# Summing the seven Strassen products of two feed-forward stages in PSUM, with operand sums prepared in other stages

## The chip, the cores and the metric

The kernel runs on one core of one Trainium2 chip. The metric is the device time of one execution in microseconds (us), the median of several runs. A core has a matrix engine (TensorE, PE in the profile), VectorE (DVE), ScalarE (ACT) and GpSimd (POOL); SyncE (SP) issues the DMA transfers between the chip's main memory and the on-chip memory, SBUF. TensorE writes its results into PSUM, eight banks of 128 partitions by 512 float32; GpSimd and the DMA engines do not read it.

## What is computed

Two decoder layers on 1024 tokens of width 1024, in float32. Each has a token mixing part (one input projection, four groups of heads A to D, one output projection) and a gated feed-forward part of inner width 2816:

```python
def conv_glu_ffn(h, w_gate, w_up, conv_w, w_down):
    gate = causal_dwconv(h @ w_gate, conv_w)
    return (jax.nn.gelu(gate, approximate=True) * (h @ w_up)) @ w_down

for l in range(DEPTH):
    h = rms_norm(x, pre_mix_g[l])
    ...
    x = x + rms_norm(mix, post_mix_g[l])
    h = rms_norm(x, pre_ffn_g[l])
    y = conv_glu_ffn(h, w_gate[l], w_up[l], conv_w[l], w_down[l])
    x = x + rms_norm(y, post_ffn_g[l])
```

## The kernel before

**Products.** A float32 product is taken as three matmuls (`mm3`, lines 208 to 212): every operand is split into a rounded part and a remainder in the float32r type, and hi·hi, hi·lo and lo·hi are added up in PSUM. `split` (line 195) makes the parts: a cast on ScalarE (L197) and a subtraction (L198) on GpSimd, or on VectorE where the call says so.

Both feed-forward stages use Strassen's scheme in Winograd's form. A and B are cut into 2 x 2 blocks, and seven products take the place of eight:

```python
#   S1 = A21 + A22, S2 = S1 - A11, S3 = A11 - A21, S4 = A12 - S2,
#   T1 = B12 - B11, T2 = B22 - T1, T3 = B22 - B12, T4 = B21 - T2,
#   P = A11 B11, S2 T2, A12 B21, S3 T3, A22 T4, S1 T1, S4 B22 (in the order they are taken),
#   U2 = P0 + P1, U3 = U2 + P3, C11 = P0 + P2, C21 = U3 + P4, C22 = U3 + P5, C12 = U2 + P5 + P6.
```

**Stages of a layer.** The input projection (`proj_d`, then `group_d`, `proj_c`, `proj_a`, `proj_b`, gates) takes feature tiles of 48 matmuls each; a tile's weight is loaded by `load` (L192) and split by ScalarE and GpSimd one or two tiles ahead. Group D's chunks run among the projections. Then come the groups A to C, the output projection and the two stages in question.

**Up stage** (`ffn1`, line 1229). A is the normed stream h (halves of tokens and of features). B is one tile f of 128 inner features, its gate and its up weights, for 22 tiles. `seq` lists (tile, product); every product is 12 matmuls of 512 columns into a PSUM bank of its own (pool pd, four banks). `prep` runs six products ahead: `operand_b` (line 1209) makes T1 to T4 on GpSimd, L1213, and `split` the two parts. After a product VectorE adds it to what came before (L1328: into u2, u3, z); ScalarE copies product 0 to p1 (L1337). `conv` runs the three taps of the convolution on VectorE (L1301, L1303) and the gelu on ScalarE, and L1334 multiplies gate by up. One tile of the gated result, 512 KB, is stored to gd. At the start, `combine_s2` and `combine_a` make the sums S1 to S4 of the stream and their parts; A5 takes the slot of s2 and so waits until S4 has been made.

**Down stage** (`ffn2`, line 1379). A is the gated result, B the weights wdn. The first tile is taken plainly by 48 matmuls. Nine pairs of tiles follow, in three groups of three (`PAIRS`); for a group each of the seven products is summed over its three pairs in four banks (one for each 128 tokens of a half) and then added by VectorE into acc or y in SBUF (L1395, in `op`). VectorE also makes S1 to S4 of each pair and GpSimd T1 to T4 (`operand_b`), four operands ahead (`NLA2`), from loads of 1 MB. The last three tiles are taken plainly by token tile, 18 matmuls each, with the post norm (`squares`, `rstd2`, `post_res`) and, in layer 0, the next layer's pre norm and its transposes (`prenorm_steps`, L219) following each token tile.

The order on each engine is fixed by a scheduler when the kernel is built; each engine takes its instructions in that order and waits on semaphores. Buffers are pools with a number of slots: a load or a write waits until the slot's last reader is done.

## Time and profile before

| | us |
|---|---|
| median of 3 runs | 3053.49 (3052.45 to 3054.06) |
| profiled execution, span | 3048.2 |
| TensorE busy | 2770.0 (91%) |
| VectorE busy | 2041.5 (67%) |
| GpSimd busy | 1690.1 (55%) |
| ScalarE busy | 1226.0 (40%) |

The span is that of one profiled execution, from its first to its last instruction. Matmuls are pipelined in the profile: one of 512 columns is shown with 0.39 us though the next starts 0.23 us later, so a busy TensorE isn't TensorE at its peak. "Clock" is the share of TensorE's full clock that the chip granted. A group of rows joins instructions of one line, operation and shape; "idle before, releaser" is the time in which the engine had waited, and whose instruction ended the wait. Names are those of the program's tiles without their numbers.

In layer 0 the up stage runs from about 787 to 1245 us and the down stage to about 1537; in layer 1 from 2306 to 2764 and to 3037.5.

### The profile page before, as it was taken

The numbers are of one execution on the slowest core, as the hardware profiler recorded it, in microseconds if no ns is written. First come the engines' busy times: TensorE is split into PE (matmuls) and PEld (weight loads), VectorE is DVE, ScalarE is ACT, GpSimd is POOL, SyncE is SP. The second block draws the span as 40 slices with busy tenths as digits, with TensorE's granted clock in tenths as the row PEclk, the third lists the DMA queues.
The fourth block names the chain that finished last, engine by engine and source line by source line (L and its number), as shares of the span: only waits on it lengthen the run. The fifth ranks groups of instructions, "written<-read, shape, count | busy, mean of one in ns | idle before, by whom it ended". The sixth has DMA issues, their size and how long they took to land. (4 is left out here: it accounts for less than half of the span.)

```text
span 3048.2 us, 39804 instructions
## 1 busy us (share of the span) xinstructions
PE 2770.0 (91%) x14952; PEld 2236.5 (73%) x14952; DVE 2041.5 (67%) x2866; ACT 1226.0 (40%) x2342; POOL 1690.1 (55%) x1362
## 2 busy tenths in 40 slices
PE   7999998999699999788899999989996999998878
PEld 6787775777588888666677877757775888886666
DVE  5564328863887777867855633388649877777787
ACT  4423437455433333333344234374544333334332
POOL 2121234546888887567631212344468988876684
PEclk9999999999899999889999999999998999999999
DMA  3221331124222222322222213311242222213223
GB/s 119 68 87 49 113 123 53 52 91 145 76 99 81 83 80 73 132 83 83 90 85 75 86 46 113 117 59 46 98 139 83 104 77 83 78 68 118 90 76 131
DMA packets 93551, 270.62 MB, mean 89 GB/s; under 512 B 17296, under 2 KB 28848, under 8 KB 93360
## 3 DMA queue, kind: packets, MB, share of 16 engines
q1 hardware_dynamic: 93360, 268.09, 25.6%
q8 instruction: 118, 1.93, 0.3%
q14 instruction: 73, 0.60, 0.1%
HBM read 203.50 MB, written 64.55 MB: 88 GB/s over the span
## 5 line engine op out<-in xcount | busy, mean ns | idle before, releaser
L198 POOL TENSOR_TENSOR wr<-wst,wr 128x512 fp32r<-128x512 f32 (+1 forms) x260 | 460.4, 1778 | 561.9 <-ACT wr L197 542.8
L211 PE MATMUL pd<-h,wr 128*128 128x512 f32 x1216 | 483.9, 398 | 0.6 <-DVE h L198 0.6
L210 PE MATMUL pd<-h,wr 128*128 128x512 f32 x1040 | 417.1, 401 | 0.0
L212 PE MATMUL pd<-h,wr 128*128 128x512 f32 x1040 | 414.2, 398 | 0.0
L197 ACT CAST wr<-wst 128x512 fp32r<-128x512 f32 (+1 forms) x262 | 198.1, 760 | 426.5 <-POOL wst L1213 131.7
L211 PEld LDWEIGHTS pd<-h,wr 128*128 128x128 f32 x1216 | 229.9, 189 | 54.0 <-issue 3.1
L1303 DVE SCALAR_TENSOR_TENSOR g<-z,pp,g 128x512 f32<-128x512 f32 x176 | 236.2, 1342 | 13.7 <-POOL z L1298 2.6
L210 PEld LDWEIGHTS pd<-h,wr 128*128 128x128 f32 x1040 | 195.8, 188 | 46.9 <-issue 5.1
L212 PEld LDWEIGHTS pd<-h,wr 128*128 128x128 f32 x1040 | 195.7, 188 | 44.0 <-issue 1.9
L210 PE MATMUL pd<-wr,h 128*128 128x256 f32 x640 | 185.5, 290 | 0.0
L211 PE MATMUL pd<-wr,h 128*128 128x256 f32 x640 | 184.8, 289 | 0.0
L212 PE MATMUL pd<-wr,h 128*128 128x256 f32 x640 | 184.5, 288 | 0.0
L210 PE MATMUL pd<-h 128*128 128x512 f32 x312 | 129.2, 414 | 59.0 <-DVE y L1395 52.5
L198 POOL TENSOR_TENSOR wr<-ust,wr 128x512 fp32r<-128x512 f32 x88 | 142.5, 1620 | 51.1 <-ACT wr L197 50.9
L215 PE MATMUL pm<-g,g 128*128 128x128 f32 (+1 forms) x672 | 118.2, 323 | 29.3 <-issue 12.9
L211 PE MATMUL pd<-hs,wr 128*128 128x512 f32 x352 | 139.0, 395 | 0.4 <-DVE hs L198 0.4
L210 PE MATMUL pd<-hs,wr 128*128 128x512 f32 x352 | 139.0, 395 | 0.0
L212 PE MATMUL pd<-hs,wr 128*128 128x512 f32 x352 | 138.6, 394 | 0.0
L215 PEld LDWEIGHTS pm<-g,g 128*128 128x128 f32 x672 | 97.0, 198 | 56.4 <-issue 30.9
L211 PE MATMUL pd<-h 128*128 128x512 f32 x312 | 127.1, 407 | 3.9 <-POOL h L198 3.9
L210 PEld LDWEIGHTS pd<-wr,h 128*128 128x128 f32 x640 | 125.6, 196 | 2.3 <-ACT t L378 1.5
L212 PE MATMUL pd<-h 128*128 128x512 f32 x312 | 126.3, 405 | 0.0
(418 smaller groups left out, 7422.1 us busy)
## 6 DMA issues: line engine op xcount, KB each, us to landing
wst<-in_wgu_dram SPq DMA_DIRECT2D x44, 512.0 KB, 3.5
ust<-in_wgu_dram SPq DMA_DIRECT2D x44, 512.0 KB, 3.5
gd<-g SPq DMA_DIRECT2D x44, 512.0 KB, 2.6
wst<-in_wfm_dram SPq DMA_DIRECT2D x32, 512.0 KB, 3.6
wst<-in_wo_dram SPq DMA_DIRECT2D x32, 512.0 KB, 3.6
x<-x SPq DMA_DIRECT2D x24, 512.0 KB, 4.2
wst<-in_wtm_dram SPq DMA_DIRECT2D x20, 512.0 KB, 3.6
h<-gd SPq DMA_DIRECT2D x10, 1024.0 KB, 7.9
```

The source lines that it names most:

```text
L197: self.marks["hi"] = self.nc.scalar.copy(out=hi, in_=src)
L198: (eng or self.nc.gpsimd).tensor_tensor(out=lo, in0=src, in1=hi.bitcast(F32), op=ALU.subtract)
L210: mm(out, lhsT=a[0], rhs=b[0], start=start, stop=False)
L211: mm(out, lhsT=a[0], rhs=b[1], start=False, stop=False)
L212: return mm(out, lhsT=a[1], rhs=b[0], start=False, stop=stop)
L215: self.nc.tensor.matmul(out, lhsT=lhsT, rhs=rhs, start=start, stop=stop)
L1303: nc.vector.scalar_tensor_tensor(out=c, in0=x[:, j:j + 512], scalar=w(j), in1=c, op0=ALU.mult, op1=ALU.add)
```

## The change

- `mm3` gets an argument `onto`, for adding onto a bank that has been read already.
- **Up stage.** Product 0 and then 1, 3 and 4 are added up in one bank (`pa`), products 5 and 6 in another (`pc`); ScalarE copies the bank after products 0, 1, 3 and 4, VectorE reads PSUM for products 2, 6 and 3 or 5. `seq` is in a new order that puts a product of another tile, or another bank, between two that share one. From the 13th product on, the remainder of five of the seven weight operands is made by VectorE instead of GpSimd. `combine_a` makes the parts of A5 earlier and in another slot. `store` writes the gated result of two tiles as the seven operands A11, S2, A12, S3, A22, S1, S4 (256 KB each), with four sums on VectorE; the last two tiles are written plainly.
- **Weight operands of the down stage.** `down_sums`, ten steps in each layer, run in the projection stage: two loads of 512 KB, four subtractions on GpSimd, two stores of 512 KB to td.
- **Down stage.** Ten pairs and two plain tiles. The product is the outer loop (0, 2, 1, 5, 6, 3, 4), the pairs the inner one; products 0, 1, 3, 4 share the four pm banks, 2 has pd banks, 5 and 6 share pd banks. The banks are emptied once per product. A class `Back` prepares operands, four ahead: two loads of 256 KB into a staging slot (four slots), one cast and one subtraction of 128 x 1024. The last six operands are taken by token tile. The next layer's norms use pd banks.

```diff
+    def mm3(self, out, a, b, start, stop, onto=False):
+        mm = lambda x, y, **k: self.nc.tensor.matmul(out, lhsT=x, rhs=y, skip_group_check=onto, **k)
...
+        self.td, self.sums = self.down_sums(l)
         cx = self.proj_c(l, hT, misc)
...
             self.proj_fm(l, hT, (AQ0 + i, evac))
+            next(self.sums, None)
...
-            A[3], A[4] = ((fr("f1", "hs", 4), fr("f1", "hs", 4)) for _ in range(2))
+            A[3], A[5] = ((fr("f1", "hs", 4), fr("f1", "hs", 4)) for _ in range(2))
...
-        seq = [(f, i) for i in (0, 2) for f in range(NFB)] + [(f, i) for f in range(NFB) for i in (1, 3, 4, 5, 6)]
-        seq += [(f, i) for f in range(NFB, NF) for i in range(7)]
+        seq = [(0, 0), (1, 0), (0, 2), (1, 2), (0, 1), (0, 3), (0, 5), (1, 1), (0, 4), (0, 6), (1, 5), (1, 3)]
+        for f in range(2, NF):
+            seq += [(f, 0), (f - 1, 4), (f - 1, 6), (f, 2), (f, 1), (f, 5), (f, 3)]
+        seq += [(NF - 1, 4), (NF - 1, 6)]
...
-            self.split(w[:, 0, :], w[:, 1, :], self.operand_b(i, *B[f]), nc.vector if j in LOV else None)
+            self.split(w[:, 0, :], w[:, 1, :], self.operand_b(i, *B[f]), nc.vector if j in LOV or j > 12 and i not in (0, 2) else None)
...
+            op(s1, a21, a22, ALU.add)
+            op(a21, a11, a21, ALU.subtract)
+            op(s2, a22, a21, ALU.subtract)
+            op(s4, a12, s2, ALU.subtract)
+            for i, x in ((1, s2), (3, a21), (5, s1), (6, s4)):
+                out(i, x)
...
+            if i == 0:
+                p = pa[f] = self.ps([128, 512], "pd" if f < 2 else "pm")
+            elif i == 5:
+                p = pc[f] = self.ps([128, 512], "pm" if f < 2 else "pd")
+            elif i == 2:
+                p = self.ps([128, 512], "pd")
+            else:
+                p = pc[f] if i == 6 else pa[f]
...
+            if i in (0, 1, 3):
+
+                x = xs[f, i] = self.t("f0", "x", 6, [128, 512])
+                nc.scalar.copy(out=x, in_=p)
+                if i == 3 and f in pc:
+                    nc.vector.tensor_tensor(out=x, in0=pc[f], in1=x, op=ALU.add)
...
-            for t in range(4):
-                self.mm3(ps[t], tuple(A[:, e, t * 128:(t + 1) * 128] for e in range(2)),
-                         tuple(B[:, e, :] for e in range(2)), k == 0, k == len(groups[gi]) - 1)
-                if k < len(groups[gi]) - 1:
-                    continue
...
-                    op(dve, x(i), x(i), ps[t], ALU.add)
...
+            for t in range(4):
+                self.mm3(banks[which][t], (X[:, 0, t * 128:t * 128 + 128], X[:, 2, t * 128:t * 128 + 128]),
+                         (X[:, 1, :], X[:, 3, :]), k and i in (0, 2, 5), stop, i in (1, 3, 4, 6))
+            if not stop:
+                continue
+            for t in range(4):
+                p = banks[which][t]
+                if i == 0:
+                    nc.scalar.copy(out=y[t][:, lo], in_=p)
+                elif i == 2:
+                    add(y[t][:, lo], p, y[t][:, lo])
+                    half(t, 0)
...
+            for p in range(NP):
+                w = [self.t("p1", "d", ND) for _ in range(2)]
+                for e in range(2):
+                    nc.sync.dma_start(out=w[e], in_=self.I["wdn"][l, 2 * p + e])
+                (b11, b12), (b21, b22) = ((x[:, 0:512], x[:, 512:1024]) for x in w)
+                sub = lambda o, x, y: nc.gpsimd.tensor_tensor(out=o, in0=x, in1=y, op=ALU.subtract)
+                sub(b11, b12, b11)
+                sub(b12, b22, b12)
+                sub(b22, b22, b11)
+                sub(b21, b21, b22)
+                for e in range(2):
+                    nc.sync.dma_start(out=td[p][:, 2 * e:2 * e + 2, :].rearrange("p a b -> p (a b)"), in_=w[e])
+                yield
...
+        self.seq = [(i, u) for i in (0, 2, 1, 5, 6, 3, 4) for u in pairs + (tail if i in (2, 6, 4) else [])]
...
+        r = b.t(*(("st", "st", 4) if self.more else ("w", "wst", 2)), [128, 2, 512])
...
+            dma(out=r[:, 0, :], in_=a)
+            dma(out=r[:, 1, :], in_=w)
+            X = b.t(*(("u", "u", NUL) if i == 4 else ("h", "h", 8)), [128, 4, 512], F32R)
+            b.split(X[:, 0:2, :], X[:, 2:4, :], r, b.nc.vector)
...
+NP, NU, NUL, NFIN = 10, 4, 4, 6
```

**What moves, on VectorE in the down stage of layer 0.** Before, at the end of a product of the first group. The rows with L1395 on r, h and ext are operand sums, L198 remainders, and y with pd the adds of the finished banks:

```order
L1395 TENSOR_TENSOR ext_10382<-r_10383 128x512
L1395 TENSOR_TENSOR r_10383<-r_10383 128x512
L1395 TENSOR_TENSOR h_10323<-h_10323,h_10322 128x512
L198 TENSOR_TENSOR h_10366<-h_10322,h_10366 128x512
L1395 TENSOR_TENSOR h_10325<-h_10325,h_10322 128x512
L1395 TENSOR_TENSOR r_10383<-r_10383,ext_10382 128x512
...
L198 TENSOR_TENSOR wr_10585<-ext_10382,wr_10585 128x512
L198 TENSOR_TENSOR wr_10605<-h_10323,wr_10605 128x512
L1395 TENSOR_TENSOR y_10380<-y_10380,pd_10567 128x512
L1395 TENSOR_TENSOR y_10380<-y_10380,pd_10568 128x512
```

After, at the end of product 2 (L198 on h and st is the remainder of one whole operand, L1452 the add of a bank, L232 a step of the norm):

```order
L198 TENSOR_TENSOR h_10887<-st_10884,h_10887 128x1024
L198 TENSOR_TENSOR h_10929<-st_10926,h_10929 128x1024
L198 TENSOR_TENSOR h_10947<-st_10944,h_10947 128x1024
L1452 TENSOR_TENSOR y_10482<-pd_10688,y_10482 128x512
L198 TENSOR_TENSOR h_10965<-st_10962,h_10965 128x1024
L232 TENSOR_SCALAR s_1963_10903<-s_1963_10903 128x1
L1452 TENSOR_TENSOR y_10483<-pd_10689,y_10483 128x512
```

The operand sums are gone from this place, and the remainders, of twice the size, stand one to an operand.

**On SP in the projection stage of layer 0.** wst is a weight of the projections (wst_3154 before and wst_3215 after is that of the second query tile of group A); C and A are stores of projected tiles, d loads of wdn and td stores of its sums. Before:

```order
L192 DMA wst_3081<-in_wfm_dram 128x1024
L1045 DMA od_1063<-do_2025 128x256
L697 DMA t_2910<-in_tab_dram 64x1024
L702 DMA kr_2915<-t_2909 64x1024
L192 DMA wst_3154<-in_wfm_dram 128x1024
L387 DMA C_2917<-t_2746 128x1024
```

After:

```order
L387 DMA C_2948<-t_2826 128x1024
L1528 DMA td_2687<-d_3117 128x1024
L1528 DMA td_2687<-d_3118 128x1024
L387 DMA A_3127<-t_3040 128x1024
L1520 DMA d_3190<-in_wdn_dram 128x1024
L1520 DMA d_3191<-in_wdn_dram 128x1024
L387 DMA A_3127<-t_3043 128x1024
L387 DMA A_3127<-t_3054 128x1024
L1528 DMA td_2687<-d_3190 128x1024
L1528 DMA td_2687<-d_3191 128x1024
L192 DMA wst_3215<-in_wfm_dram 128x1024
```

This weight stood ahead of the stores of C; it now stands behind them, three stores of A and the stores of two steps of sums.

**On TensorE at the end of layer 0's down stage.** jh is the normed row of a token tile, transposed (L219) for the next layer; pd with h and wr is the first projection of that layer, pm and pd with u the last products. Before:

```order
L210 MATMUL pd_12381<-h_11846,wr_12377 128x512
L219 MATMUL pm_12286<-cf,jh_12272 128x128 x4
L219 MATMUL pm_12293<-cf,jh_12272 128x128 x4
L211 MATMUL pd_12381<-h_11847,wr_12377 128x512
L212 MATMUL pd_12381<-h_11846,wr_12378 128x512
```

After:

```order
L209 MATMUL pd_12142<-wr_11934,u_11912 128x512 x3
L219 MATMUL pd_12153<-cf,jh_12110 128x128 x4
L219 MATMUL pd_12160<-cf,jh_12110 128x128 x4
L219 MATMUL pd_12181<-cf,jh_12167 128x128 x4
L219 MATMUL pd_12188<-cf,jh_12167 128x128 x4
L219 MATMUL pd_12202<-cf,jh_12195 128x128 x4
L219 MATMUL pd_12209<-cf,jh_12195 128x128 x4
L209 MATMUL pd_12244<-h_11525,wr_12240 128x512
```

The transposes of the last three token tiles stood among projection matmuls and now stand in a row ahead of the first of them.

## Rows read from the trace of the kernel before

**Rows 1.** Busy time by stretch: start of the up stage of layer 0, its steady part, its down stage; the down stage of layer 1 and what follows it. Columns: stretch, its length, busy us (and instructions) of PE, PEld (weight loads), DVE, ACT and POOL, granted clock, DMA share, GB/s.

```profile
787.00:833.00 46.00, 20.88 (x81) 15.08 (x79) 44.65 (x34) 15.25 (x29) 42.53 (x29) 0.79 0.14 51
833.00:1245.00 412.00, 411.72 (x1767) 333.20 (x1767) 313.74 (x335) 131.12 (x218) 325.09 (x263) 0.99 0.26 90
1245.00:1537.00 292.00, 237.52 (x987) 188.94 (x986) 228.59 (x263) 113.56 (x210) 199.35 (x138) 0.91 0.25 91
...
2764.00:3037.50 273.50, 231.04 (x946) 184.07 (x944) 213.24 (x236) 99.88 (x183) 188.08 (x125) 0.93 0.25 94
3037.50:3048.20 10.70, 0.37 (x2) 0.00 (x0) 6.09 (x10) 1.62 (x6) 2.65 (x4) 0.76 0.46 162
```

**Rows 2.** Waits of TensorE: tile and line that waited, what it waited for, us in total, times, longest; first two rows from 1245 to 1556 us (layer 0), last two from 2764 to the end (layer 1).

```profile
PE pd L210 <- DVE y L1395: 33.8, 7, 9.7
PE pd L210 <- DVE acc L1395: 13.6, 4, 5.6
...
PE pd L210 <- DVE y L1395: 23.0, 6, 9.7
PE pd L210 <- DVE acc L1395: 11.4, 4, 5.6
```

**Rows 3.** At the end of a product in layer 0's down stage: busy time by stretch from 1271 to 1281 us (columns as in rows 1), then from the timeline of VectorE: start, us, engine, line, operation, output and inputs.

```profile
1271.00:1281.00 10.00, 10.00 (x46) 8.23 (x45) 10.00 (x6) 5.59 (x10) 10.00 (x7) 1.00 0.01 2
...
1279.43 1.78 DVE L1395 TENSOR_TENSOR r<-r,ext 128x512 f32<-128x512 f32 x1
...
1289.68 0.68 DVE L198 TENSOR_TENSOR wr<-h,wr 128x512 fp32r<-128x512 f32 x1
1290.28 2.47 DVE L1395 TENSOR_TENSOR y<-y,pd 128x512 f32<-128x512 f32 x4
```

**Rows 4.** From the timeline of TensorE, in the steady up stage (the first and the last of twelve rows) and around the same end of a product (in brackets the idle time before it and who ended it); and the stretch from 1285.5 to 1295 us, columns as in rows 1.

```profile
999.63 0.39 PE L210 MATMUL pd<-hs,wr 128*128 128x512 f32 x1
...
1002.16 0.39 PE L212 MATMUL pd<-hs,wr 128*128 128x512 f32 x1
...
1281.10 0.39 PE L212 MATMUL pd<-h 128*128 128x512 f32 x1
...
1291.01 0.79 PE L210 MATMUL pd<-h 128*128 128x512 f32 x1 [9.52 <-DVE y L1395]
...
1285.50:1295.00 9.50, 3.99 (x9) 3.14 (x10) 7.82 (x12) 0.00 (x0) 3.57 (x3) 0.50 0.00 0
```

**Rows 5.** Groups of instructions by line, kept apart by shape: operation, output and inputs, shapes, count | busy us, mean ns of one | idle before. First row and third from 1290 to 1500 us, the others from 860 to 1240.

```profile
L1395 DVE TENSOR_TENSOR y<-y,pd 128x512 f32<-128x512 f32 x48 | 30.0, 677 | 2.9 <-PE pd L212 2.9
L198 DVE TENSOR_TENSOR g<-gr,g 128x1024 fp32r<-128x1024 f32 x1 | 1.2, 1226 | 3.0 <-ACT g L197 3.0
L1493 ACT COPY acc<-pd 128x512 f32<-128x512 f32 x8 | 4.6, 587 | 0.3
L197 ACT CAST wr<-wst 128x1024 fp32r<-128x1024 f32 x1 | 1.1, 1050 | 0.0
```

**Rows 6.** DMA: GB/s in 40 equal slices of the stretch from 1245 to 1505 us, and loads with their count, KB each and median us from issue to landing (the first in the projection stage, the second in layer 0's down stage).

```profile
GB/s 8 165 422 142 3 0 0 0 0 0 0 304 408 258 0 0 0 0 0 3 81 1 117 405 365 4 0 0 1 0 3 0 0 0 163 0 24 301 81 0
...
t<-in_tab_dram SPq DMA_DIRECT2D x1, 256.0 KB, 3.3
...
h<-in_wdn_dram SPq DMA_DIRECT2D x3, 1024.0 KB, 9.6
```

**Rows 7.** From the timelines of VectorE and TensorE at the end of layer 0's down stage: the add of the last token tile, the last transposes, the next projection matmul and the 48th.

```profile
1543.34 0.67 DVE L1395 TENSOR_TENSOR y<-y,pd 128x512 f32<-128x512 f32 x1
...
1554.05 1.07 PE L219 MATMUL pm<-cf,jh 128*128 128x128 f32 x8
1554.87 0.48 PE L211 MATMUL pd<-h,wr 128*128 128x512 f32 x1
...
1555.88 0.39 PE L212 MATMUL pd<-h,wr 128*128 128x512 f32 x1
```

**Rows 8.** Groups of VectorE in the steady up stage, 860 to 1240 us, columns as in rows 5.

```profile
L1303 DVE SCALAR_TENSOR_TENSOR g<-z,pp,g 128x512 f32<-128x512 f32 x78 | 103.4, 1326 | 6.5 <-POOL z L1298 1.3
L1328 DVE TENSOR_TENSOR u<-pd,u 128x512 f32<-128x512 f32 x79 | 52.1, 678 | 0.0
L1301 DVE TENSOR_SCALAR g<-z,pp 128x512 f32<-128x512 f32 x39 | 51.8, 1329 | 1.4
L1334 DVE TENSOR_TENSOR g<-g,u 128x512 f32<-128x512 f32 x40 | 39.1, 977 | 0.7
```

**Rows 9.** Waits of TensorE at the start of layer 0's up stage, 787 to 838 us, columns as in rows 2.

```profile
PE pd L210 <- ACT s2h L197: 12.8, 1, 12.8
PE pd L210 <- ACT s L197: 5.6, 1, 5.6
```

**Rows 10.** The projection stage of layer 0 after group D: busy time from 290 to 430 us (columns as in rows 1), and from the timelines a load of a projection weight on SP's queue, the remainder of that weight on GpSimd, and a GpSimd operation of 128 x 512 there.

```profile
290.00:430.00 140.00, 139.81 (x844) 118.74 (x844) 43.03 (x52) 52.52 (x72) 37.62 (x23) 1.00 0.26 89
...
314.89 0.34 SPq L192 DMA_DIRECT2D wst<-in_wfm_dram  x1
...
340.13 3.38 POOL L198 TENSOR_TENSOR wr<-wst,wr 128x1024 fp32r<-128x1024 f32 x1 [6.99 <-ACT wr L197]
...
400.59 1.30 POOL L408 TENSOR_TENSOR t<-gt,rbh 128x512 f32<-128x512 f32 x1 [0.83 <-DVE gt L407]
```

More of the change, by code (lines that the diff above doesn't have):

```diff
@@ L630, in proj_a @@
             self.proj_fm(l, hT, (AQ0 + i, evac))
+            next(self.sums, None)
             tiles.append(self.spill("A", [q, k, f2]))
@@ L640, in proj_b @@
             self.proj_fm(l, hT, (m, self.copy_half(t)))
+            next(self.sums, None)
         wgk = self.t("p1", "wgk", 1, [16, 128])
@@ L666, in proj_c @@
             self.proj_fm(l, hT, (m, self.copy_half(t)))
+            next(self.sums, None)
             ts.append(t)
@@ L1078, in mixing @@
         bG = self.gate(l, TBG, hT, self.rbh[:, RB_B:RB_B + 64], True)
+        next(self.sums, None)
         dG = self.gate(l, TDZ, hT, self.rbh[:, RB_D:RB_D + 64], True)
+        for _ in self.sums:
+            pass
         self.close("p1", "h", "w")
@@ L1378, in ffn1 @@
[L1378 to L1387 removed]
+                nc.vector.tensor_tensor(out=g[f, 1], in0=g[f, 1], in1=xs[f, 3], op=ALU.mult)
+            elif i == 6:
+                add(xs[f, 1], xs[f, 1])
+                nc.vector.tensor_tensor(out=g[f, 0], in0=g[f, 0], in1=xs[f, 1], op=ALU.mult)
+                store(f)
@@ L1524, in ffn2, with half, finish @@
+        g_post, g_pre = gb
+        late, behind, ss, hT = [], [], {}, None
+        def half(t, n):
+            if t not in ss:
+                ss[t] = self.t("c", "s2", 8, [128, 2])
+            self.squares(y[t], n, ss[t], self.t("f", "fc", 1, None, BF16))
+            c = (lo, hi)[n]
+            (dve if last and n else pool).tensor_tensor(out=y[t][:, c], in0=y[t][:, c], in1=g_post[:, c], op=ALU.mult)
+        def finish(t, ev):
+            nonlocal hT
+            half(t, 1)
             behind[:] = [self.last_sq]
@@ new lines, in ffn2 @@
+        rest = [(i, back.take()) for i, _ in seq[n_last:]]
+        for t in range(4):
+            tk = slice(t * 128, t * 128 + 128)
+            p = banks["pm"][t]
+            n = sum(i == 4 for i, _ in rest)
+            for k, (i, X) in enumerate(rest[:n]):
+                self.mm3(p, (X[:, 0, tk], X[:, 2, tk]), (X[:, 1, :], X[:, 3, :]), False, k == n - 1, True)
+            nc.scalar.copy(out=y[4 + t][:, lo], in_=p)
+            half(4 + t, 0)
+            p = self.ps([128, 512], "pd")
+            for k, (i, W) in enumerate(rest[n:]):
+                X = rest[n - (NF - 2 * NP) + k][1]
+                self.mm3(p, (X[:, 0, tk], X[:, 2, tk]), (W[:, 0, :], W[:, 1, :]), k == 0, k == len(rest) - n - 1)
+            finish(4 + t, add(y[4 + t][:, hi], p, y[4 + t][:, hi]))
```

326 lines of the change are left out of this document (132 added, 194 removed).

## The prediction

> **What bounds the kernel now.** I read the stage windows first [rows 1]. They show one engine that works nearly all the time in some stages and is held up in others, so a single share for the whole kernel says little. In the long part of the up stage TensorE is busy 411.7 of 412 us, at a granted clock of 0.99, while VectorE has 313.7 and GpSimd 325.1: that stage is TensorE's own. The start of the up stage has 20.9 us of TensorE work in 46, with VectorE and GpSimd both full. In the down stage TensorE is busy 237.5 of 292 us in layer 0 and 231.0 of 273.5 in layer 1, and the clock falls to 0.91 and 0.93. The waits of TensorE there [rows 2] come almost wholly from VectorE's adds of finished products into y and acc, 47.4 us in layer 0 and 34.4 in layer 1. VectorE isn't short of time on average; it is late at the moments when a group of products ends. At one of them [rows 3], a run of operand sums and remainders stands ahead of the add: six operations take 10 us beside seven of GpSimd's, that is 1.67 us each where one alone takes 0.68, and the four adds begin only at 1290.28, 9 us after the last matmul's start [rows 4]. Then the next matmuls run at the lower of the two clock levels, 1.2 instead of 2.4 GHz: busy 3.99 us for nine, at a granted 0.50 [rows 4]. So each such wait is paid for twice.
>
> **Matmul pace.** At full clock twelve matmuls of 512 columns start between 999.63 and 1002.16, one per 0.23 us, though each is shown as 0.39 [rows 4]. Over the steady up stage 1768 matmuls take 409 us (412 at a mean clock of 0.99, less some 3 for what the clock costs in its first microseconds) [rows 1], 0.2314 each, and I use that.
>
> **Down stage, the matmuls.** Before, a layer has 48 for the first tile, 756 for nine pairs and 144 for three tail tiles, 948. After, 10 pairs by 7 products by 12 is 840, two tail tiles in four places make 96: 936. At 0.2314 that is 216.6 us.
>
> **Down stage, the waits.** The product is now outermost, and four banks are emptied once per product instead of three times. 84 adds per layer become about 24 evictions, split between ScalarE and VectorE. VectorE's operand sums are gone: the gated operands are summed in the up stage and the weight operands while the projections run. What is left per operand (12 matmuls, 2.73 us at 0.2275) is one cast of 128x1024 on ScalarE, 1.05 us, and one subtraction of the same size on VectorE, 1.23 us [rows 5]. Neither is full, and GpSimd has little to contend with. There remain two changes of product where the next product adds onto banks that have just been filled (5 to 6, 3 to 4). A bank is needed again some 2.1 us after its last matmul (nine matmuls on the other three lie between), a copy takes 0.59 us and an add 0.68 [rows 5], so the cover is thin but there; if VectorE is late again, each costs up to the 9.5 us of [rows 4]. With 1 us for the last operands, whose slots turn over slowly, I take 4 us a layer, with ends of 0 and 20. It is nearest to a wait without queued operand sums ahead, since the order after shows three subtractions ahead of such an add, all for operands whose loads run ahead, where it showed a row of operand sums.
>
> **Down stage, the loads.** Each operand needs two loads of 256 KB in 2.73 us, 192 GB/s, where bursts of the stage now reach 400. A 256 KB load lands after 3.3 us, the 1 MB weight loads, several at a time, after 9.6 [rows 6]. The Trainium skill, DMA: Bandwidth & Descriptors (Measured), advises against this size: it asks for 1 MiB transfers for three quarters of the peak, where the kernel goes from 1 MB to 256 KB. By its table (138 GB/s at 64 KB, 341 at 1 MB) an estimate for two of 256 KB sent one by one would be 1.5 to 3.8 us, on both sides of 2.73; the landing rows here speak against it, since they show less time per load and several in flight. The first four operands are loaded under the up stage, so I put no wait at the change of stage.
>
> **End of layer 0.** Before, the transposes of the last three token tiles stand between projection matmuls, which fill the wait for the norm. After, all of them stand ahead of the first projection matmul, so TensorE idles for the norm's chain. In the trace of before the chain from the last add (1543.34) to the last transposes (1554.05) is 10.7 us [rows 7]; with the step from matmul to add and the transposes I take 12, and 3 more for the clock after it (about 2 lost in nine matmuls [rows 4], the rest in transposes). Layer 0 from 1245 to the end of the 48th projection matmul (1555.88 plus 0.23) takes 311 us; after: 216.6, 40 earlier transposes at 0.10 (8 in 0.82 us [rows 7]) 4, waits 4, idle 12, 48 projection matmuls 11, clock 3, together 250.6. **Gain 60.4.** Layer 1 from 2764 to 3037.5 takes 273.5; after 216.6 and 4: **gain 52.9.** The last 10.7 us stay, as the last token tile is finished by the same steps.
>
> **Up stage, steady part.** TensorE has 84 matmuls a tile in both, 19.4 us. VectorE per tile now reads PSUM 3 times instead of 7, but takes over five remainders from GpSimd and two sums for the pair form: 15 operations that read SBUF alone and 3 that read a bank. GpSimd keeps 6 large ones of 11 to 12. An operation with a PSUM operand takes 0.678 us beside GpSimd's work; those that read SBUF alone take 0.98 to 1.33 [rows 8]. Without neighbours 15 by 0.68 and 3 by 0.68 are 12.2 us. If each of GpSimd's six holds up one of VectorE's by the whole difference between 1.70 and 0.68, 6.1 are added: 18.4, still under 19.4. ScalarE is busy 131 of 412 us [rows 1] and gets three more copies of 0.59 us a tile, 8 us of 19.4 in all. A bank that is added onto again has one whole product (2.73 us) between ScalarE's copy and the next use. So I put the steady part at no change.
>
> **Up stage, start.** Of the waits the 12.8 us for s2h stays, and the 5.6 us for s goes [rows 9], since A5 no longer lies in s2's place; some of that is taken by work that moves earlier. Gain 4 a layer, between 0 and 6: 8 in all.
>
> **Projection stage.** This is where the weights' sums go: per layer 20 loads and 20 stores of 512 KB on SP and 40 subtractions on GpSimd, at 1.30 us each 52 us [rows 10]. GpSimd is busy 37.6 of 140 us there, so the sum fits; the order is the cost. On SP a store waits for the four subtractions, which wait for their loads, and the next projection weight is queued behind the store. TensorE never waits there now and is busy 139.8 of 140 us. Before, a weight is asked for at 314.89 whose remainder is made at 340.13, some 25 us ahead; after, that lead is used up by the two steps ahead of it, and the remainder itself stands behind four subtractions, 5.2 us. One weight, that of the second query tile, would by this chain come 2 us late; the others come just in time. I take 3 a layer, ends 0 and 20: **loss 6.**
>
> **Sum.** 60.4 + 52.9 + 8 - 6 = 115.3. On the profiled execution, 3048.2 us of span plus the 5.3 that lie around it to the median of 3053.5, that is 2932.9 + 5.3 = **2938 us**. At the good ends (no waits, start 6 each, no loss in the projections, pace 0.2275) it is some 2910; with 10 us of waits more in each layer and stage 2965.
>
> **Rivals.**
> (a) Slower: VectorE becomes the bound of the up stage. Now 8 SBUF operations a tile take 1.24 us in the mean (4 at 1.326, 2 at 1.329, 2 at 0.977 [rows 8]). If all 15 take that, a tile needs 15 x 1.24 + 2 = 20.6 us, TensorE waits 1.2 in each of 44 tiles, +53: 2991. The whole gain is used up at 22.0 us a tile, a mean of 1.33; from there on the kernel is slower, and at 1.45, halfway to the 1.67 of [rows 3], it is 15 x 1.45 + 2 = 23.8, +194: 3132. For it: the start of the up stage shows both engines full and slow. Against it: those rows have as many operations of GpSimd as of VectorE, and it now has 6 against 15. The Trainium skill speaks for this rival: Perfetto Trace Analysis (Optimizing Scalar/DVE Operations) warns that work moved between these two engines may not help, since they share a read port; SBUF — State Buffer (Who interferes with whom) makes it a lock that blocks the other engine for a whole instruction. The 0.678 us rows with one SBUF operand agree with the second page. Chance 0.10.
> (b) The projections are held by the queue: 10 to 20 us a layer, 2953 to 2972. For it: SP's order. Against it: GpSimd's slack. 0.13.
> (c) The ring of four staging buffers turns over too slowly: at 9.6 us to landing plus 1.05 and 1.23, a quarter of it is 2.97 us per operand instead of 2.73, 78 times in each layer +19, 2976; it decides from 8.6 us. 0.06.
> (d) The sums in PSUM don't free TensorE: ScalarE's copy is queued behind a gelu that waits for three steps of the convolution (4 us), 1.3 us beyond the product of cover, 44 times: +57, 2995. 0.07.
> My forecast has 0.64.
>
> **Range and chances.** The forecast, (b), (c) and part of (a) and (d) reach from 2905 to 2995. About 0.2% (6 us) can be told from no change. Faster 0.90; same 0.02 and slower 0.08, all of it from (a).
>
> **What would show it.** Right: no wait above 3 us and a clock near 1 in both down stages, TensorE busy over 95% there; VectorE at 260 to 390 of 412 us in the up stage with TensorE full; one idle stretch of some 8 to 13 us before the projections of layer 1. Wrong: waits for remainders of wr on VectorE in the up stage (a), for wst or wr in the projections (b), for st from DMA in the down stage (c), for copies of x by ScalarE (d).

## The result and the profile after

The changed kernel takes 2968.02 us (median of 4 runs, 2962.82 to 2971.51) beside 3053.23 of the kernel before: a ratio of 0.9721 [0.9708, 0.9735]. The forecast was 2938 with a range of 2905 to 2995. The profiled execution has a span of 2964.6 us, 83.6 less than before.

The stages come first again, as in [rows 1] and [rows 10]: the projections of layer 0 after group D, the steady up stage and the down stage of layer 0, and the down stage of layer 1. Columns as there.

```profile
290.00:448.00 158.00, 147.88 (x850) 123.20 (x850) 55.05 (x53) 52.76 (x72) 96.06 (x62) 0.94 0.59 208
862.00:1262.00 400.00, 399.89 (x1726) 323.69 (x1725) 303.64 (x373) 150.76 (x266) 179.66 (x155) 1.00 0.31 104
1262.00:1490.00 228.00, 220.19 (x981) 179.53 (x979) 133.37 (x146) 107.70 (x143) 30.41 (x26) 1.00 0.65 208
2744.00:2956.40 212.40, 212.40 (x935) 175.05 (x933) 118.11 (x121) 95.90 (x121) 16.98 (x14) 1.00 0.67 219
```

The down stages are now TensorE's own: busy 220 of 228 and 212.4 of 212.4 us at full clock, where before it was 81 and 84% at 0.91 and 0.93. The price stands in the first row: 148 of 158 us at 0.94, where before nothing was lost.

The waits of TensorE answer to [rows 2] and [rows 9] (columns as there). First the projections of layer 0 (290 to 450 us), then the start of its up stage (804 to 862), then its down stage and the change of layer (1262 to 1510). Layer 1's down stage and the steady up stage have none to list.

```profile
PE pm L215 <- ACT gt L685: 3.8, 2, 3.2
PE pd L209 <- ACT wr L197: 3.7, 1, 3.7
PE pd L209 <- POOL wr L198: 2.5, 2, 1.3
...
PE pd L209 <- ACT s2h L197: 12.8, 1, 12.8
PE pm L209 <- DVE x L1375: 5.8, 1, 5.8
...
PE pd L219 <- DVE jh L286: 14.5, 5, 7.0
...
PE pm L209 <- DVE y L1452: 1.0, 2, 0.7
```

The 47 and 34 us of waits for VectorE's adds are down to 1.0. The largest block left in the down stage is the chain of norms at its end, 14.5 us.

From the start of equal pieces of work in the two profiled executions comes this ledger (us, + is time gained; "projections" runs to the first matmul of group A's attention, "down" to the 48th projection matmul of layer 1 or to the last matmul):

| stage | predicted | layer 0 | layer 1 |
|---|---|---|---|
| projections | -3 each | -17.5 | -16.5 |
| up | +4 each | -2.2 | -1.4 |
| down | +60.4, +52.9 | +55.5 | +62.5 |
| last 10.7 us | 0 | | +2.3 |

With +0.8 from the stages between, that is 83.5 of the 83.6. In the changed kernel four matmuls of each down stage run before its border, among the last of the up stage, and count there (0.9 us). One term is far off: the projections, 34.0 us instead of 6.

**Two stalls in the projections.** From the timelines of SP, VectorE and TensorE: the rope table's load and its first use, and the second query tile's weight.

```profile
307.18 1.25 SPq L1520 DMA_DIRECT2D d<-in_wdn_dram  x2
308.48 0.52 SPq L701 DMA_DIRECT2D t<-in_tab_dram  x1
...
315.95 2.34 DVE L702 TENSOR_TENSOR t<-misc,t 64x1024 f32<-64x1024 f32 x1 [12.97 <-DMA t<-in_tab_dram]
318.33 1.64 DVE L693 SCALAR_TENSOR_TENSOR ckv<-ckv,pp,gt 128x512 f32<-128x512 f32 x1
...
320.68 2.07 PE L215 MATMUL pm<-gt,ones 128*128 128x512 f32 x2 [3.21 <-ACT gt L685]
...
353.94 2.55 SPq L1528 DMA_DIRECT2D td<-d  x2
356.58 0.41 SPq L192 DMA_DIRECT2D wst<-in_wfm_dram  x1
...
362.52 1.04 ACT L197 CAST wr<-wst 128x1024 fp32r<-128x1024 f32 x1 [9.30 <-DMA wst<-in_wfm_dram]
...
363.62 1.22 PE L209 MATMUL pd<-h,wr 128*128 128x512 f32 x2 [3.68 <-ACT wr L197]
```

The table, asked for behind a step's loads of wdn at 308.48 (305.01 before), lands after 7.4 us (3.3 in [rows 6]). VectorE takes its instructions in order, so the step of the norm on which ScalarE and then TensorE depend stands behind the table's use (L693 behind L702, at 318.33). The second stall is the one that the forecast named: the weight is asked for at 356.58 (314.89 before, [rows 10]), behind stores that wait for GpSimd's subtractions, and TensorE waits 3.68 and 1.21 us. The weight after it costs another 1.29 us. Layer 1 has the same stalls: 3.60 us at the table, 4.68 and 1.21 at the second query tile's weight, 0.57 and 2.22 at the next. With the two large stalls the clock falls. Windows of the stretches at these two, after the wait at the start of the up stage and around the change of layer, with columns as above:

```profile
319.20:329.40 10.20, 8.18 (x14) 4.64 (x15) 6.17 (x5) 3.96 (x6) 7.62 (x6) 0.51 0.64 204
360.00:370.20 10.20, 5.37 (x12) 3.79 (x13) 5.99 (x4) 1.54 (x2) 6.55 (x4) 0.52 0.57 220
855.00:861.80 6.80, 4.19 (x10) 3.32 (x11) 6.80 (x8) 2.63 (x5) 4.11 (x4) 0.52 0.26 77
1493.70:1510.70 17.00, 6.83 (x25) 5.82 (x25) 10.88 (x15) 6.03 (x14) 8.16 (x15) 0.50 0.31 101
```

All four are at the lower level, 1.2 GHz. The first three go with waits of 3.2, 3.7 and 5.8 us and last 7 to 10 us; the fourth holds two waits, of 7.0 and 3.2 us.

Of layer 0's 17.5 us some 10 are waits, and about 7 are the lower clock (an estimate: half of the time in the first two stretches in which TensorE was not waiting).

### The profile page after: what moved, and what is told of

It is laid out like the page before. It is cut to its first block, busy times and chain, and to the rows that moved or that the text cites. A ratio compares the mean times of both kernels' runs of the same rounds, so it can differ in the third digit from the quotient of the medians.

```text
span 2964.6 us, 40009 instructions
## 1 busy us (share of the span) xinstructions
PE 2743.4 (93%) x14928; PEld 2223.9 (75%) x14928; DVE 1881.0 (63%) x2740; ACT 1272.3 (43%) x2338; POOL 1192.4 (40%) x1008
## 5 line engine op out<-in xcount | busy, mean ns | idle before, releaser
L209 PE MATMUL pd<-h,wr 128*128 128x512 f32 x2624 | 664.8, 404 | 14.9 <-ACT wr L197 8.9
L198 POOL TENSOR_TENSOR wr<-wst,wr 128x512 fp32r<-128x512 f32 (+1 forms) x176 | 336.1, 1912 | 772.7 <-ACT wr L197 771.4
L209 PE MATMUL pd<-wr,h 128*128 128x256 f32 x1920 | 248.1, 290 | 1.1 <-issue 1.1
L209 PE MATMUL pm<-h,wr 128*128 128x512 f32 x848 | 235.2, 401 | 11.8 <-DVE x L1375 11.7
L198 DVE TENSOR_TENSOR h<-st,h 128x1024 fp32r<-128x1024 f32 x120 | 152.6, 1273 | 122.6 <-ACT h L197 119.8
L209 PEld LDWEIGHTS pm<-h,wr 128*128 128x128 f32 x848 | 162.0, 191 | 52.2 <-DVE x L1375 12.5
L209 PE MATMUL pd<-wr,f 128*128 128x512 f32 x768 | 186.1, 399 | 11.4 <-POOL wr L198 10.5
L209 PE MATMUL pd<-h 128*128 128x512 f32 x816 | 185.6, 389 | 0.0
L209 PEld LDWEIGHTS pd<-wr,f 128*128 128x128 f32 x768 | 143.6, 189 | 45.4 <-POOL wr L198 12.2
L209 PEld LDWEIGHTS pd<-h 128*128 128x128 f32 x816 | 153.2, 188 | 31.8
L209 PE MATMUL pm<-h 128*128 128x512 f32 x720 | 165.6, 390 | 0.8 <-DVE h L198 0.8
L1311 DVE SCALAR_TENSOR_TENSOR g<-z,pp,g 128x512 f32<-128x512 f32 x176 | 152.7, 868 | 7.3
```

The costliest lines, as they stand in the source:

```text
L198: (eng or self.nc.gpsimd).tensor_tensor(out=lo, in0=src, in1=hi.bitcast(F32), op=ALU.subtract)
L209: mm = lambda x, y, **k: self.nc.tensor.matmul(out, lhsT=x, rhs=y, skip_group_check=onto, **k)
L1311: nc.vector.scalar_tensor_tensor(out=c, in0=x[:, j:j + 512], scalar=w(j), in1=c, op0=ALU.mult, op1=ALU.add)
```

## The experiments

Theory after the result: the 34 us are those of the sums' DMA and order in the projections (rival (b)), and the gain of the down stage comes from fewer readings of the banks together with the sums' absence. Each ratio is to the kernel before on the same chip; where a difference to the changed kernel is given, it is that of two ratios times 3053 us, since the runs were spread over several chips.

**1. What the weights' sums cost.** No sums at all:

```diff
-            for p in range(NP):
...
+            return
+            yield
...
-        return a, self.td[u][:, {5: 0, 3: 1, 4: 2, 1: 3}[i], :]
+        return a, w[l, 2 * u + (i > 3)][:, lo if i in (1, 4) else hi]
```

> The sums of the weights are left out of the projection stage altogether: no loads, subtractions or stores there, and the down stage reads wdn in place of td, so its output isn't that of the reference. Theory (these sums alone cost the projection stages their 17.5 and 16.5 us): the time falls by 30 to 36 us from 2968, to about 2934, with the projection stage ending 17 us earlier in each layer. Rival (something else in the stage moved): less than 15 us, 2953 or more.

Measured: 2933.29 us, 0.9601 [0.9587, 0.9616]: 37 us less. From 290 to 436 us TensorE is busy 145.8 of 146.0 at full clock: in the projections after group D the whole of the loss is the sums'. By the stages of the profiled execution 31 of the 34 us are back. Layer 1 even ends 2.4 us ahead of the kernel before; layer 0 stays 5.4 us behind it. It is behind by about that much at the start of group D already (the first transposes there start at 207.8 us, and at 203.0 in the two other kernels), and it makes no sums at all.

**2. Traffic or the wait for GpSimd.** The loads and stores stay.

```diff
-                sub(b11, b12, b11)
-                sub(b12, b22, b12)
-                sub(b22, b22, b11)
-                sub(b21, b21, b22)
```

> All 20 loads and 20 stores per layer stay in their places, the 40 subtractions of GpSimd are left out, so td holds the weights as they are and the output isn't that of the reference. Theory (the loss is a matter of the DMA queue: the rope table's load and one weight's load come late): most of the loss stays, 2955 to 2968. Rival (GpSimd's subtractions, in front of the remainders and of the stores, are the cause): as without any sums, about 2934.

Measured: 2951.39, 0.9662 [0.9645, 0.9678]: 18 us less, half. Neither of the two stalls is left. That alone doesn't clear the traffic: without subtractions the steps run earlier, and only 11 of a layer's 20 loads of wdn still fall between 290 and 440 us in layer 0, at 164 GB/s. A new stretch at the lower clock appears as well, in group D. The window of this run, and then that of the changed kernel (columns as above):

```profile
228.00:241.70 13.70, 13.70 (x80) 10.21 (x77) 1.79 (x4) 3.38 (x10) 0.76 (x3) 0.50 0.43 143
```

```profile
228.00:241.70 13.70, 13.61 (x125) 10.56 (x124) 6.16 (x20) 4.34 (x14) 2.04 (x7) 1.00 0.29 98
```

TensorE does 80 matmuls there instead of 125, and the next layer shows the same from 1699 on. Before it stands a wait of 1.4 us for VectorE's C (L896) that the changed kernel doesn't have. That stretch is some 6 us of layer 0's loss. So neither side was cleanly right.

**3. The stores one step late**, so that none stands on SP ahead of its subtractions:

```diff
+            old = None
+            for p in range(NP + 1):
...
+                if old is not None:
+                    for e in range(2):
+                        nc.sync.dma_start(out=td[p - 1][...], in_=old[e])
+                old = w
```

> The stores of each step of sums are written one step later, when their subtractions are long done; nothing is left out. Theory of the queue's order (weights wait behind stores that wait for subtractions): the stall at the second query tile's weight goes, 6 to 10 us per layer, 2948 to 2956; the stall at the rope table stays. Rival (landing times under the heavier traffic, not the order, make the loads late): within 5 us of 2968.

Measured: 2962.86, 0.9693 [0.9679, 0.9708]: some 8 us less in all by the ratios (3.5 in the profiled execution, nearly all of it in layer 0's projections), where 6 to 10 a layer were expected. The weight goes out at 350.70 instead of 356.58 and its stall is 1.8 instead of 3.7, but the waits for remainders on GpSimd grow from 2.5 to 4.2 us, and the table's stays at 2.25.

**4. The table ahead of the sums.** Its load is issued before the first step of `down_sums`.

```diff
+        self.tab = self.pt()
+        nc.sync.dma_start(out=self.tab[64:128], in_=self.I["tab"][64:128])
...
-        nc.sync.dma_start(out=tab[64:128], in_=self.I["tab"][64:128])
+        tab = self.tab
```

> The rope table is loaded before the first step of sums; nothing is left out. Theory (its late landing holds VectorE's queue at the key's rotation, behind which the norm's scaling and then TensorE wait): the first stall and the half clock after it go, 8 us per layer, about 2952, and more if the weights' loads also move forward in the queue. Rival (the stall comes from ScalarE or GpSimd): within 3 us of 2968.

Measured: 2956.74, 0.9672 [0.9656, 0.9688]: 15 us less by the ratios, 8 in the profiled execution. The wait for gt is gone and of the second stall 2.5 us are left. But group D gets the stretch at the lower clock here too (230 to 243.6 us, granted 0.51), behind a wait of 1.8 us, and in layer 0 that eats the gain: its projections lose 17.3 us instead of 17.5, layer 1's 9.8 instead of 16.5.

**5. The end of layer 0.** The last transposes go to pm banks, and the scheduler then puts them among projection matmuls:

```diff
-                late.append(self.prenorm_steps(t, x, g_pre, hT, "f", behind, bank="pd"))
+                late.append(self.prenorm_steps(t, x, g_pre, hT, "f", behind, bank="pm" if t > 4 else "pd"))
```

> The transposes of the last three token tiles of layer 0's down stage use pm banks instead of pd banks, so that projection matmuls, which use pd banks, can be placed between them. Theory (TensorE is idle 17 us there and at the lower clock afterwards only because the banks' ring forces the order): 10 to 14 us fall away, about 2956. Rival (the norm's chain holds the next layer's first projections whatever the order): within 3 us of 2968.

Measured: 2958.18, 0.9696 [0.9677, 0.9715]: some 8 us less by the ratios; in the profiled execution the way from layer 0's up stage to the 48th projection matmul of layer 1 is 10.3 us shorter, as expected. The waits for jh that were 7.01 and 3.16 us are 1.21 and 2.69, and 17.1 us at the lower clock become 3.4.

**6. The start of the up stage.** The parts of A6 are made after the first tile's fifth product.

```diff
-            for i, x in ((4, a22), (6, a12)):
...
+                if f == 0:
+                    for k in range(4):
+                        self.split(*(o[:, k, :] for o in A[6]), a12[:, k, :], nc.vector)
```

> At the start of the up stage the four remainders of A6 are written behind the add of product 5 of the first tile, not ahead of it. Theory (that add, which now has to read the bank before product 6 goes onto it, is queued behind A6's remainders on VectorE): the 5.8 us wait and the half clock after it shrink, 4 to 8 us per layer, 2952 to 2960. Rival (product 6 then waits as long for A6 itself): within 3 us of 2968.

Measured: 2962.5, 0.9706 [0.9683, 0.9728]: about 5 us less, which the interval doesn't tell from nothing. The wait of 5.8 us for VectorE's add (L1375) becomes 1.9, with a new one of 2.2 for h; in the profiled execution the up stages are 1.4 and 2.3 us shorter.

**7. The remainders back on GpSimd**, by the condition of the kernel before:

```diff
-... nc.vector if j in LOV or j > 12 and i not in (0, 2) else None)
+... nc.vector if j in LOV else None)
```

> The remainders of the up stage's weights go back to GpSimd. Theory (the steady up stage is TensorE's on either split): within 4 us of 2968, the stage 400 us as now, VectorE busy about 250 of it and GpSimd 300. Rival (the move from GpSimd to VectorE was needed to keep TensorE fed): 10 us or more slower.

Measured: 3011.34, 0.9864 [0.9847, 0.988]: 44 us more. My theory of no change fell. The steady part from 862 to 1285 us (columns as above), the longest of TensorE's waits in it, and the chain at one of the ten, from the timelines of GpSimd, VectorE, ScalarE and TensorE:

```profile
862.00:1285.00 423.00, 405.31 (x1719) 325.04 (x1719) 292.16 (x273) 149.36 (x268) 316.99 (x258) 0.99 0.30 99
```

```profile
PE pm L209 <- ACT x L1379: 17.7, 10, 3.4
```

```profile
1017.44 0.38 POOL L1306 COPY z<-z 128x2 f32<-128x2 f32 x1
1017.78 1.75 POOL L198 TENSOR_TENSOR wr<-wt,wr 128x512 fp32r<-128x512 f32 x1
...
1016.27 1.50 DVE L1309 TENSOR_SCALAR g<-z,pp 128x512 f32<-128x512 f32 x1
1017.70 0.68 DVE L1328 TENSOR_TENSOR h<-g,h 128x512 f32<-128x512 f32 x1
1018.30 2.56 DVE L1311 SCALAR_TENSOR_TENSOR g<-z,pp,g 128x512 f32<-128x512 f32 x2
...
1020.90 0.63 ACT L1312 ACTIVATE g<-g 128x512 f32<-128x512 f32 x1 [7.13 <-DVE g L1311]
...
1021.94 0.58 ACT L1379 COPY x<-pm 128x512 f32<-128x512 f32 x1
...
1022.58 0.50 PE L209 MATMUL pm<-h,wr 128*128 128x512 f32 x1 [1.64 <-ACT x L1379]
```

GpSimd is busy 317 of 423 us and no engine is full over the stretch, but VectorE is without a pause from 1004.96 to 1020.86. Its three steps of the convolution (L1309, L1311), beside GpSimd's remainders, take 1.50 and 2.56 us; the gelu waits for them, and ScalarE's copy of the bank stands behind the gelu. TensorE waits 1.64 us, once for each pair of tiles. GpSimd's copy of two columns (L1306), which the convolution needs too, isn't what is late: it is done at 1017.82, and in all twenty cases of the two layers L1311 starts when VectorE's step before it ends, with no idle time. At the same place in the changed kernel GpSimd is idle from 1000.71 to 1005.84 us, and VectorE's three steps read:

```profile
1000.59 0.47 DVE L1309 TENSOR_SCALAR g<-z,pp 128x512 f32<-128x512 f32 x1
...
1001.59 0.74 DVE L1311 SCALAR_TENSOR_TENSOR g<-z,pp,g 128x512 f32<-128x512 f32 x1
...
1002.85 0.73 DVE L1311 SCALAR_TENSOR_TENSOR g<-z,pp,g 128x512 f32<-128x512 f32 x1
```

This is rival (d)'s mechanism (a gelu behind three steps of 4 us; priced at 1.3 us 44 times, here 1.6 some 20 times, with a stretch at the lower clock after the first), brought about by rival (a)'s slow steps; moving the remainders away from GpSimd is what kept it out.

The Trainium skill, Perfetto Trace Analysis (Optimizing Scalar/DVE Operations), warns that moving work between these two engines may not help. Here it is worth 44 us. Nor did VectorE pay on the whole: beside the emptier GpSimd its steps of the convolution shrank from the 1326 and 1329 ns of [rows 8]. Its products of gate and up, which in the timeline run beside GpSimd's sums, went from 977 to 1421 and 1727 ns (groups of the changed kernel, 862 to 1262):

```profile
L1311 DVE SCALAR_TENSOR_TENSOR g<-z,pp,g 128x512 f32<-128x512 f32 x83 | 70.6, 850 | 3.5
L1393 DVE TENSOR_TENSOR g<-g,x 128x512 f32<-128x512 f32 x21 | 36.3, 1727 | 0.1
...
L1309 DVE TENSOR_SCALAR g<-z,pp 128x512 f32<-128x512 f32 x42 | 20.2, 481 | 29.2 <-ACT z L1391 29.2
```

**8. The banks read three times as often.** After the third and the sixth pair of a product VectorE also reads the four banks, into scratch, as often as when a group had three pairs:

```diff
+            extra = u in (2, 5)
...
+            if extra:
+                for t in range(4):
+                    add(junk, banks[which][t], gb[0][:, lo])
```

> In the down stage VectorE also reads the four banks after the third and the sixth pair of each product, into scratch, and the next pair's matmuls go on in them: three reads per product as before, with the sums of operands still made elsewhere. Theory (the waits came from operand sums queued ahead of the adds, not from the number of adds): under 10 us more in both layers together, 2968 to 2978. Rival (emptying the banks less often is what took the waits away): 1 to 2 us for each of 14 more readings per layer, 2990 to 3020.

Measured: 2999.84, 0.9822 [0.9808, 0.9837]: 31 us more, some 15 a layer. The theory (under 10 us) fell; the rival's price held. Waits of TensorE in the two down stages:

```profile
PE pm L209 <- DVE junk L1452: 9.8, 3, 5.8
...
PE pm L209 <- DVE junk L1452: 9.5, 3, 5.2
```

**9 and 10. The operand sums beside the down stage again**, into scratch. First with the staging slot as input, then with an operand's finished slot and a constant:

```diff
+            if self.more and u < NP:
+                for e, n, x in ((b.nc.vector, {1: 2, 5: 1, 6: 1}, self.junk[0]), (b.nc.gpsimd, {1: 2, 3: 1, 4: 1}, self.junk[1])):
+                    for _ in range(n.get(i, 0)):
+                        e.tensor_tensor(out=x, in0=r[:, 0, :], in1=r[:, 1, :], op=ALU.subtract)
```

```diff
-                        e.tensor_tensor(out=x, in0=r[:, 0, :], in1=r[:, 1, :], op=ALU.subtract)
+                        e.tensor_tensor(out=x, in0=self.src[:, 0:512], in1=X[:, 0, :], op=ALU.subtract)
```

> Beside the down stage of the changed kernel the operand sums are made a second time, into a scratch tile that nobody reads: for each of ten pairs four subtractions of 128x512 on VectorE and four on GpSimd, as many as the kernel before made there per pair. Everything else, the output too, is as in the changed kernel. Theory (moving the sums away is a large part of the gain, since VectorE was late at the end of a product because of them): waits of TensorE on VectorE come back, 15 us or more per layer, and the time is 2995 us or more. Rival (with banks emptied once per product VectorE's lateness has lost its place, so the sums could have stayed beside the stage): VectorE has some 40 x 1.3 = 52 us more work in a stage where it was busy 131 of 226, TensorE waits at most 5 us more per layer, 2968 to 2978.

> The eighty added sums of the run before (sums beside the down stage, into scratch, read by nobody) again, as many and as long, on the same engines and behind the same operands, but read from an operand's finished slot (eight of them) and a constant, not from the staging slot. The output is still that of the changed kernel. In the trace of the run before, the staging loads start late: a slot is free only when VectorE's and GpSimd's sums have read it, ScalarE's casts then wait for the load, and its copy of a bank stands behind them in the queue, for which TensorE waited 9.4 us. Theory (the sums cost time there because they hold the ring of four staging slots, not because the engines lack the time): the waits go, 2968 to 2980. Rival (VectorE with 40 x 0.7 to 1.0 us more, and GpSimd beside it, is late by itself): 2995 to 3012.

Measured: 3012.66, 0.9866 [0.9851, 0.9881], 44 us more, as the theory had it; and 2993.82, 0.9797 [0.9774, 0.982], 23 more (16 to 30 by its interval). The longest waits of TensorE in layer 0's down stage ahead of the norms at its end, in the first run and then in the second:

```profile
PE pd L209 <- ACT y L1481: 9.4, 1, 9.4
PE pm L209 <- DVE h L198: 6.2, 5, 2.6
```

```profile
PE pm L209 <- DVE h L198: 7.8, 5, 3.0
PE pd L209 <- ACT y L1482: 2.8, 1, 2.8
```

And the cause of the 9.4, from ScalarE's timeline in the first run: its casts wait for staging loads, and the copy of four finished banks stands behind them.

```profile
1396.11 1.05 ACT L197 CAST h<-st 128x1024 fp32r<-128x1024 f32 x1 [1.92 <-DMA st<-in_wdn_dram]
1398.41 1.05 ACT L197 CAST h<-st 128x1024 fp32r<-128x1024 f32 x1 [1.26 <-DMA st<-in_wdn_dram]
1399.36 2.04 ACT L1481 COPY y<-pd 128x512 f32<-128x512 f32 x4
```

The second run was meant to decide between the ring of staging slots and the engines' own time, and landed between the two (its forecasts were 2968 to 2980 and 2995 to 3012): about half of the 44 us goes, and 23 stay with sums that don't touch the ring. The half that goes is not the ring's alone beyond doubt, since the edit also moves the sums from ahead of an operand's cast and subtraction to behind them. In that run VectorE is busy 175 of 238 us, and its remainder of an operand takes 1386 ns in the mean instead of 1273, beside GpSimd's sums of 1880.

**11 and 12. The edits together.** 4, 5 and 6 in one kernel; then 3 as well.

> The changed kernel with three edits at once that were each measured alone: the table of the rope loaded before the sums, the transposes of the last token tiles in pm banks, the parts of A6 made after the first tile's fifth product. If the effects add (they lie in different stages): 2968 less about 13, 10 and 5, that is 2940, 2933 to 2948. If they don't (a stall that one edit takes away is replaced by the next one in the same queue), 2950 to 2962.

> The same three edits and the stores of the weights' sums one step late. Theory (after the table's stall the second query tile's weight, queued behind a store that waits for GpSimd, is what is left of the queue's price): 4 to 8 us less than the three edits alone, 2930 to 2944. Rival (the traffic itself and the half clock in group D's stage set what is left): within 3 us of the three edits alone.

Measured: 2943.25, 0.9643 [0.9627, 0.9658], and 2933.91, 0.961 [0.9592, 0.9628]. The three nearly add up (2940 expected, 2943 measured), and the late stores, worth 8 us alone, give another 9 on the same chip. The projections of the last kernel, columns as above, and the landing of their weights:

```profile
290.00:438.70 148.70, 146.59 (x893) 123.48 (x891) 56.38 (x59) 55.71 (x81) 95.35 (x62) 1.00 0.62 220
...
wst<-in_wfm_dram SPq DMA_DIRECT2D x4, 512.0 KB, 7.3
```

Both stalls are gone at the same traffic and the same 95 us of GpSimd, with weights that land later than in the changed kernel (7.3 us instead of 5.9 in the median). So it is the order on SP that made the stalls, and not the traffic or the landing times by themselves. This is the fastest version that still makes the sums in the projections, some 120 us below the kernel before. Its projections still lose 6.4 and 5.5 us. Layer 1's are group D's stretch at the lower clock, which this kernel has there too, behind a wait of 1.8 us:

```profile
1685.10:1698.80 13.70, 13.70 (x81) 9.97 (x80) 1.99 (x5) 3.48 (x10) 0.76 (x3) 0.50 0.21 64
```

## Why the prediction held, and where it was wrong

**The number.** 2968 is inside the range, but it is rival (b)'s number and not the forecast's: the range held because it had been drawn wide enough for (b). Two small terms don't come out of their words. Ten us more in each layer of one stage is 2958 and of two stages 2978, not 2965. And the 5.3 us around the span are mostly the distance of that execution from the median: around the changed kernel's profiled execution lie 1.8 us (2966.38 beside 2964.6).

**Down stage: right.** 113.3 us were forecast and 118.0 measured, by two errors of opposite sign, so the closeness of the sum is partly luck. Layer 1 came out 9.6 us better: the 4 us of waits did not come at all, and the pace was 0.2272, the good end, not 0.2314, another 4. I had taken the pace of the up stage, which is 0.2317 there now too (400 us for 1726 matmuls); in the down stage of the kernel before matmuls already start 0.227 us apart at full clock (1296 to 1334 us). Layer 0 came out 4.9 worse, at the change of layer: from the last matmul to the first projection matmul TensorE needs 17 us where I took 12, with 17.1 us at the lower clock. The chain from the last add to the last transposes was costed right, 10.0 us instead of 10.7. Left out was the way to that add. It comes 5.6 us after the last matmul (1490.26), behind VectorE's steps for the token tile before:

```profile
1492.48 3.38 DVE L328 SCALAR_TENSOR_TENSOR y<-y,rs,x 128x1024 f32<-128x1024 f32 x1
...
1495.84 0.67 DVE L1452 TENSOR_TENSOR y<-pd,y 128x512 f32<-128x512 f32 x1
```

The kernel before shows the same, 6.1 us from its last matmul (1537.21) to the add at 1543.34 [rows 7]; I read the chain from the add on.

**Where that gain comes from** the prediction gave as two causes in one. Runs 8 to 10 price each alone, put back into the changed kernel: tripled readings cost 31 us, sums 23 without the ring and 44 with it. If they add, that is 54 to 75 of 118; the rest (the weight of 1 MB loads, the order of operands) was not taken apart. By TensorE's time, estimated from the waits and the granted clock of the two traces, some 80 of the 118 us are waits that went and some 23 the lower clock; the rest is fewer matmuls (12 a layer) and their pace.

**The loads: right.** 256 KB loads land after 3.1 to 4.0 us (medians) in layer 0's down stage, at 208 GB/s, and TensorE waits for none. The advice of 1 MiB per transfer in the Trainium skill, DMA: Bandwidth & Descriptors (Measured), would have spoken against this size. With several in flight it gave the 192 GB/s that the stage needs; a stage that needs more, no run here shows.

**Up stage, steady: right.** TensorE is busy 399.9 of 400 us, VectorE 303.6, inside the 260 to 390 given. Rival (a) is out: VectorE's operations on SBUF alone take 0.90 us in the mean (276.1 us for 307), not the 1.24 that (a) needs, as GpSimd's work fell from 325 to 180 us. The prediction put this at no change and so missed that it was worth 44 us not to leave the remainders where they were (run 7).

**Up stage, start: wrong sign, small.** The wait of 5.6 us for s is gone, as forecast, and one of 5.8 for an add has come: the bank of product 5 must be read before product 6 goes onto it, and the read stands behind eight remainders of A4 and A6 and two steps of the convolution on VectorE. I had priced the wait that goes and not the one that a shared bank brings.

**Projections: the step that failed.** "One weight, that of the second query tile, would by this chain come 2 us late; the others come just in time. I take 3 a layer" should have been 17. The weight was late as said, by 3.7 and 1.2 us instead of 2 in layer 0. Missed were three things. The rope table is on the same queue, and its use stands on VectorE ahead of a step that TensorE waits for. The weight after the second query tile's wasn't just in time either, 1.3 us late in layer 0 and 2.8 in layer 1. And the lower clock with each large stall, priced everywhere else, was not priced here. Loads did land later under traffic of 208 instead of 89 GB/s (weights of 512 KB after some 6 us instead of 3.6, the table after 7.4 instead of 3.3), and that is part of each stall; but run 12, where they land later still, has none. Rival (b), 10 to 20 us a layer and 2953 to 2972, had mechanism and price, and its sign, waits for wr in the projections, is what came; it should have had the larger chance.

**Open.** Group D falls to the lower clock in both layers of runs 2, 4 and 11, and in run 12 in layer 1 alone, though in layer 0 of run 12 the same wait of 1.8 us stands before it. What decides is not settled. Nor is what layer 0's projections still lose in run 12, 6.4 us. Of these, 6.2 are there by 310 us, ahead of where the two stalls were, and run 1 loses 5.4 without any sums, so a loss of this size can arise without them. The order of the earlier work may differ between these kernels; that was not tested.

## What to carry to other kernels

When work is moved into a stage that has slack, follow every other load on the queue that it joins, not the tightest one alone: what stands ahead of it decides when it goes out, and a late small load can hold an in-order engine on which the critical one depends. Price each wait of TensorE with the stretch at half clock that goes with it. And ask of two engines that are far from full what each does while the other works: here where five remainders a tile are made was worth 44 us, by three steps of the convolution that were slow at the wrong moment.

## What the runs showed of the hardware

Two things I had not expected. Stretches at half clock come after waits as short as 1.4 us, yet not every such wait brings one: behind a wait of 1.8 us group D ran 13.6 us at 0.51 in run 4, and in run 12 at full clock in layer 0 and 13.7 us at 0.50 in layer 1. And VectorE's time for an operation goes by what GpSimd does at that moment, far more than by VectorE's own load. The same step of the convolution (L1309) took 0.47 us with GpSimd all but idle and 1.50 beside its remainders. By groups it fell from 1329 to 481 ns when GpSimd's busy share went from 79 to 45%, while VectorE's own stayed at 76%, and the products that run beside GpSimd's sums became slower; operations that read a bank stayed at 678 to 687 ns.
